# A decoder layer's up projection: products in one line, weights split four ahead, and seven of the 22 output pairs from seven half products in place of eight

## The chip, the cores and the metric

The kernel runs on one core of one Trainium2 chip. The metric is the device time of one execution in microseconds. TensorE (PE) multiplies; PEld is its weight load, which runs beside the multiplies; VectorE (DVE), ScalarE (ACT) and GpSimd (POOL) work on tiles in SBUF, the first two of them also on PSUM; SyncE (SP) issues the DMAs here.

## What is computed

One layer of a hybrid decoder: a mixing sub-layer (three kinds of attention) and a gated MLP with a causal convolution. The change lies in the MLP, in the first of its two matrix products:

```python
h = _rmsnorm(x, norm_ffn[l]) * (1.0 + sc2) + sh2          # (512, 1024)
u = _causal_dwconv(h @ w_up[l], conv_w[l], conv_b[l])     # w_up: 1024 x 5632, conv width 3
u_gate, u_val = jnp.split(u, 2, axis=-1)                  # 2816 columns each
x = x + g2 * ((jax.nn.silu(u_gate) * u_val) @ w_down[l])
```

Everything is float32.

## The kernel before

There are 512 tokens; they are the moving operand of the products, 512 columns at most. The up projection has 44 column blocks of 128; block f of the gate half and block f + 22 of the value half make a pair, and there are 22 pairs (f = 0 to 21).

To keep float32 accuracy each operand is held as a high part in the matmul's own format and a low part, the difference. So each 128x128 weight block costs three matmuls: hi x hi, lo x hi, hi x lo (lines L1290, L1291 and L1293 in `up`). One DMA brings 512 input rows of a block as a tile `w_st` (256 KB); `split_w` makes `w_hi` of it with a cast on ACT (L225) and `w_lo` with a subtraction on POOL (L227), or, where its caller asks for a share, on DVE for every second tile. A pair from f = 2 on has four such tiles and 48 matmuls of 512 columns. The first two pairs (f = 0, 1) work on 256 columns at a time, since the second half of the tokens is not there yet; they are 8 runs of 24 matmuls of 256 columns.

When a block's sum stands in PSUM, `conv` makes the convolution: one ACT operation (L1297) and two on DVE (L1298, L1299), each of which reads PSUM and one SBUF tile. A pair's end is SiLU on ACT (L1325), the product of the two halves on DVE (L1326), a cast `a_hi` on ACT (L1327) and the low part `a_lo` on DVE (L1328). These last two make the moving operand of the down projection. In its f loop the up projection also builds the gate of the residual add (`gate_steps`, L410, 16 operations on DVE in two groups, after f = 4 and f = 8).

The order on each engine is set by a scheduler that plays the program through before it runs; nothing is reordered on the chip between the instructions of DVE, ACT or POOL, so that one that waits holds those behind it. PSUM has 8 banks of 512 columns, handed out in a ring; `w_hi` and `w_lo` have 9 buffers each, `w_st` three, and the working tile `tm` eight.

## Time and profile before

| | us |
|---|---|
| median of 3 runs | 749.01 |
| lowest and highest | 748.26, 753.52 |
| profiled execution, whole | 747.43 |
| its span in the profile | 745.7 |
| busy in the span: PE | 717.4 |
| PEld | 563.3 |
| DVE | 422.4 |
| ACT | 350.5 |
| POOL | 300.1 |

The profiled execution lasted 1.73 us more than its span. Its own time is 1.58 us below the median. The up projection's f loop from pair 2 on starts at 392.51 us of the span; the down projection follows it directly.

### The profile page before, as it was taken

The page shows a single profiled execution, that of the slowest core. Times are in us where ns is not written, and L with a number is a line of the kernel's source. Part 1 is how long each engine was busy: PE and PEld are TensorE (multiplying, and loading weights), DVE is VectorE, ACT ScalarE, POOL GpSimd, SP SyncE. Part 2 cuts the span into 40 slices and gives each one's busy share as a digit, 9 for nine tenths or more (in the row PEclk, how much of TensorE's full clock was granted, in tenths as well). Part 3 has the DMA queues.
Part 4 walks back from the last instruction along what each step waited for, and adds up shares of the span by engine and source line. Part 5 has one row for each costly group of instructions (what it writes and reads, how often), then busy time and mean ns, then how long its engine had stood idle before and what let it go on. Part 6 is the DMA issues. An engine that isn't in the chain of part 4 may idle for free.

```text
span 745.7 us, 11381 instructions
## 1 busy us (share of the span) xinstructions
PE 717.4 (96%) x4224; PEld 563.3 (76%) x4224; DVE 422.4 (57%) x761; ACT 350.5 (47%) x671; POOL 300.1 (40%) x262
## 2 busy tenths in 40 slices
...
GB/s 323 394 165 42 68 19 29 86 100 225 241 193 121 63 123 44 69 46 130 82 100 127 110 178 109 202 102 93 86 102 96 88 107 103 85 99 100 86 13 113
DMA packets 43018, 86.90 MB, mean 117 GB/s; under 512 B 5001, under 2 KB 5203, under 8 KB 42963
## 3 DMA queue, kind: packets, MB, share of 16 engines
...
## 4 chain that ended last, share of the span: by engine, by line
PE 85%; DVE 9%; ACT 2%; issue 1%; DMA 1%; POOL 0%; SPq 0%; DVEq 0%; POOLq 0%; ACTq 0%
PE ch L1290 4%; PE ch L1293 4%; PE ch L1291 4%; PE mm L455 3%; PE at L1290 3%; PE at L1293 3%; PE mm L1290 3%; PE mm L1293 3%; PE at L1291 3%; PE mm L1291 3%; PE mm L456 2%; PE mm L457 2%; PE ch L374 2%; PE ch L1185 2%; PE ch L1184 2%; PE ch L1183 2%
## 5 line engine op out<-in xcount | busy, mean ns | idle before, releaser
L227 POOL TENSOR_TENSOR w_lo<-w_st,w_hi 128x512 fp32r<-128x512 f32 (+1 forms) x164 | 220.1, 1346 | 340.1 <-ACT w_hi L225 318.6
L225 ACT CAST w_hi<-w_st 128x512 fp32r<-128x512 f32 (+1 forms) x184 | 112.9, 617 | 167.9 <-PE at L1185 44.7
L227 DVE TENSOR_TENSOR w_lo<-w_st,w_hi 128x512 fp32r<-128x512 f32 x22 | 16.1, 734 | 83.8 <-ACT w_hi L225 83.8
L1290 PE MATMUL ch<-h_hi,w_hi 128*128 128x512 f32 (+1 forms) x152 | 55.2, 372 | 1.3 <-ACT h_hi L1234 1.3
L1291 PE MATMUL ch<-h_hi,w_lo 128*128 128x512 f32 (+1 forms) x152 | 54.9, 369 | 0.0
L455 PE MATMUL mm<-h_hi,w_hi 128*128 128x512 f32 x104 | 48.8, 469 | 1.8 <-ACT ptr L1017 1.8
L456 PE MATMUL mm<-h_lo,w_hi 128*128 128x512 f32 x104 | 42.2, 406 | 0.0
L457 PE MATMUL mm<-h_hi,w_lo 128*128 128x512 f32 x104 | 42.2, 405 | 0.0
L1290 PE MATMUL at<-h_hi,w_hi 128*128 128x512 f32 (+1 forms) x104 | 36.2, 360 | 0.0
L1291 PE MATMUL at<-h_hi,w_lo 128*128 128x512 f32 (+1 forms) x104 | 36.1, 359 | 0.0
L1293 PE MATMUL ch<-h_lo,w_hi 128*128 128x512 f32 (+1 forms) x152 | 35.0, 371 | 0.0
L1290 PE MATMUL mm<-h_hi,w_hi 128*128 128x512 f32 x88 | 34.7, 394 | 0.0
L1291 PE MATMUL mm<-h_hi,w_lo 128*128 128x512 f32 x88 | 34.6, 393 | 0.0
L1290 PEld LDWEIGHTS ch<-h_hi,w_hi 128*128 128x128 f32 x152 | 28.6, 188 | 7.1 <-ACT h_hi L1234 1.8
L1298 DVE SCALAR_TENSOR_TENSOR tm<-ch,vec,tm 128x511 f32<-128x511 f32 x17 | 12.7, 749 | 36.7 <-ACT tm L1297 36.7
L1291 PEld LDWEIGHTS ch<-h_hi,w_lo 128*128 128x128 f32 x152 | 28.6, 188 | 5.2
L430 DVE SCALAR_TENSOR_TENSOR w_m<-w_m,cB 128x512 f32<-128x512 f32 x32 | 25.8, 831 | 9.7 <-DMA w_m<-in_mod_cols_dram 9.6
L1293 PEld LDWEIGHTS ch<-h_lo,w_hi 128*128 128x128 f32 x152 | 26.7, 188 | 5.5 <-POOL h_lo L1235 0.2
L455 PEld LDWEIGHTS mm<-h_hi,w_hi 128*128 128x128 f32 x104 | 20.3, 195 | 9.0 <-issue 3.1
L1006 ACT ACTIVATE pr<-at,mx 128x128 f32<-128x128 f32 (+3 forms) x32 | 16.9, 527 | 21.6 <-DVE mx L1004 21.1
L1325 ACT ACTIVATE tm<-tm 128x512 f32<-128x512 f32 x22 | 13.9, 633 | 25.6 <-DVE tm L1299 25.6
L1004 DVE TENSOR_REDUCE mx<-at 128x1 f32<-128x128 f32 (+3 forms) x32 | 15.6, 488 | 17.3 <-PE at L1001 17.1
...
## 6 DMA issues: line engine op xcount, KB each, us to landing
w_st<-in_w_up_dram SPq DMA_DIRECT2D x88, 256.0 KB, 2.7
w_st<-in_w_down_dram SPq DMA_DIRECT2D x44, 256.0 KB, 2.6
...
w_m<-in_mod_cols_dram SPq DMA_DIRECT2D x32, 256.0 KB, 3.7
w_st<-in_in_cols_dram SPq DMA_DIRECT2D x30, 256.0 KB, 2.7
w_m<-in_mod_gates_dram SPq DMA_DIRECT2D x16, 256.0 KB, 3.0
w_st<-in_w_out_dram SPq DMA_DIRECT2D x16, 256.0 KB, 2.6
tm<-in_mod_gates_dram SPq DMA_DIRECT2D x16, 256.0 KB, 4.7
```

Source lines behind the costliest of these rows:

```text
L225: (V.tensor_copy if hv[0] else S.copy)(hi[:, :n], st[:, :n])
L227: e.tensor_tensor(lo[:, :n], st[:, :n], f32(hi[:, :n]), op=OP.subtract)
L374: mm(first[j], w[:, P * j:P * j + P], h[:, k, :], start=k == 0 and w is hi and not last, stop=k == NK - 1 and last)
L430: V.scalar_tensor_tensor(wm, wm, 1.0, cB[:, cols], op0=OP.mult, op1=OP.mult, accum_out=acc2[:, z, k, half:half + 1])
L455: mm(out[0], hi[:, z, :], hT_hi[:, k, :], start=k == 0, stop=False)
L456: mm(out[0], hi[:, z, :], hT_lo[:, k, :], start=False, stop=False)
L457: mm(out[0], lo[:, z, :], hT_hi[:, k, :], start=False, stop=k == NK - 1)
L1004: V.reduce_max(mx[:, 0:1], s_ps[:, :n], axis=AX.X, negate=True)
L1006: S.activation(pr[:, :n], s_ps[:, :n], AF.Exp, bias=mx[:, 0:1], accum_out=mx[:, 1:2])
L1290: mm(pu[:, tok], hi[:, k % 4, :], h2_hi[:, k, tok], start=k == 0, stop=False)
L1291: mm(pu[:, tok], lo[:, k % 4, :], h2_hi[:, k, tok], start=False, stop=False)
L1293: mm(pu[:, tok], w[k // 4][0][:, k % 4, :], h2_lo[:, k, tok], start=False, stop=k == NK - 1)
```

## The change

Pairs 0 and 1 stay. From pair 2 on the products become one list of jobs, which PE takes in the order written. A job is 12 matmuls (`product`): one weight tile, split into hi and lo, with four blocks of moving columns. Tiles are fetched seven jobs ahead and split so that, in the program's text, four split tiles are ready ahead of the one in use. The low part is now made on POOL and on DVE in turn (share 2).

Fifteen of the 22 pairs stay as they are in work: pairs 0 and 1, and 13 pairs of four jobs of 512 columns (`jobs_eight`). The other seven (5, 7, 9, 10, 12, 14, 15) are made by `jobs_seven`: the pair is seen as a 2x2 matrix of weight tiles (gate or value block, first or second half of the 1024 inputs) times a 2x2 matrix of token tiles (half of the inputs, half of the tokens), and its four quarter results come from seven products of 256 columns in place of eight. For these, sums and differences are formed:

- of the tokens once, for all seven pairs (`half_sums`): their hi and lo parts lie in four pairs of tiles `s`, `a0`, `a1`, `a2`; its 14 steps stand one behind each of the first 14 jobs;
- of the weights in each pair: four additions of 128x512 on DVE (L1357 of the new kernel), in place in four staging tiles `w_st4`, of which there are four in all; seven tiles are split per pair (one of them twice) where four were;
- of the results in each pair: four copies of 256 columns from PSUM by ACT (L1366, L1378, L1389, L1405), and three additions on DVE of 512, 256 and 256 columns (L1400, L1406, L1407). Products p6, p3 and p7 add onto a PSUM region whose value before must first have been copied out by L1366, L1378 and L1389.

The gate's steps move from behind pairs 4 and 8 to behind pairs 16 and 18.

```diff
+SEVEN = (5, 7, 9, 10, 12, 14, 15)
+NA = 16
+LA = 4
...
+    sums = [[late.tile([P, 4, 256], F32R, name=n + p) for p in ("hi", "lo")] for n in ("s", "a0", "a1", "a2")]
 
     def act_tile(arr, f):
-        return arr[0][:, f, :] if f < NK else arr[1][:, f - NK, :]
+        if f >= NA and len(arr) < 3 + (f - NA) // 2:
+            arr.append(late.tile([P, 2, T], F32R, name=f"a{(f - NA) // 2}" + ("hi" if arr is a_hi else "lo")))
+        return arr[0][:, f, :] if f < NK else arr[1][:, f - NK, :] if f < NA else arr[2 + (f - NA) // 2][:, f % 2, :]
+    def half_sums(c):
+        x = {}
+        def restore(q):
+            for h in range(2):
+                x[q, h] = tm().rearrange("p (k t) -> p k t", k=2)
+                part = (slice(0, P), slice(4 * q + 2 * c, 4 * q + 2 * c + 2), slice(256 * h, 256 * h + 256))
+                V.tensor_tensor(x[q, h], f32(h2_hi[part]), f32(h2_lo[part]), op=OP.add)
+        def combine():
+            V.tensor_tensor(x[0, 0], x[0, 1], x[0, 0], op=OP.subtract)
+            V.tensor_tensor(x[0, 1], x[1, 1], x[0, 1], op=OP.subtract)
+            V.tensor_tensor(x[1, 1], x[1, 1], x[0, 0], op=OP.subtract)
+            V.tensor_tensor(x[1, 0], x[1, 0], x[1, 1], op=OP.subtract)
+        def part(n, t):
+            hi, lo = [z[:, 2 * c:2 * c + 2, :] for z in sums[n]]
+            S.copy(hi, x[t])
+            (G if n % 2 else V).tensor_tensor(lo, x[t], f32(hi), op=OP.subtract)
+        return [lambda: restore(0), lambda: restore(1), combine] + [lambda n=n, t=t: part(n, t) for n, t in
+                                                                   enumerate(((0, 0), (1, 1), (0, 1), (1, 0)))]
+    def product(o, w, x, start):
+        hi, lo = w
+        for k in range(4):
+            mm(o, hi[:, k, :], x[0][k], start=start and k == 0, stop=False, skip_group_check=not start)
+            mm(o, lo[:, k, :], x[0][k], start=False, stop=False, skip_group_check=not start)
+        for k in range(4):
+            mm(o, hi[:, k, :], x[1][k], start=False, stop=k == 3, skip_group_check=not start)
...
+    def jobs_eight(f):
...
+        return [(lambda z=z, q=q: stage(z, q), lambda z=z, q=q: split_w(st.pop((z, q)), 2),
+                 lambda w, z=z, q=q: run(w, z, q)) for z in range(2) for q in range(2)]
+    def jobs_seven(f):
+        st, pu, snap = {}, [], []
+        def stage(z, q):
+            st[z, q] = late.tile([P, T], F32, name="w_st4", bufs=4)
+            dma(st[z, q], w_up[f + NF * z, q])
+        def parts(z, q):
+            return split_w((st[z, q], 4, T), 2)
+        def add(o, a, b, op=OP.subtract):
+            V.tensor_tensor(st[o], st[a], st[b], op=op)
+        h0, h1 = slice(0, 256), slice(256, 512)
+        a11, a12, a21, a22 = (0, 0), (0, 1), (1, 0), (1, 1)
+        def p1(w):
+            pu.extend(bank(next(ring)) for z in range(3))
+            snap.extend(tm() for z in range(2))
+            product(pu[1][:, h1], w, tokens(0, 0), True)
+            S.copy(snap[0][:, h0], pu[1][:, h1])
+        def p2(w):
+            product(pu[0][:, h0], w, tokens(1, 0), True)
+        def s5():
+            add(a11, a11, a21)
+            add(a21, a21, a22, OP.add)
+            return parts(*a21)
+        def p5(w):
+            product(pu[0][:, h1], w, combined(0), True)
+            S.copy(snap[1][:, h1], pu[0][:, h1])
+        kept22 = []
+        def s6():
+            kept22.append(parts(*a22))
+            add(a22, a22, a11)
+            return parts(*a22)
+        def p6(w):
+            product(pu[1][:, h1], w, combined(1), False)
+            S.copy(snap[0][:, h1], pu[1][:, h1])
+        def p4(w):
+            product(pu[2][:, h0], kept22[0], combined(3), True)
+        def s3():
+            add(a12, a12, a22)
+            return parts(*a12)
+        def p3(w):
+            product(pu[0][:, h1], w, tokens(1, 1), False)
+            V.tensor_tensor(pu[0], pu[0], snap[0], op=OP.add)
+            us[f].append(conv(pu[0], f))
+        def p7(w):
+            product(pu[1][:, h1], w, combined(2), False)
+            S.copy(snap[1][:, h0], pu[1][:, h1])
+            V.tensor_tensor(pu[1][:, h1], pu[1][:, h1], snap[1][:, h1], op=OP.add)
+            V.tensor_tensor(pu[1][:, h0], pu[2][:, h0], snap[1][:, h0], op=OP.add)
+            us[f].append(conv(pu[1], f + NF))
+        us[f] = []
+        none = lambda: None
+        return [(lambda: (stage(*a11), stage(*a12)), lambda: parts(*a11), p1), (lambda: stage(*a21), lambda: parts(*a12), p2),
+                (lambda: stage(*a22), s5, p5), (none, s6, p6), (none, none, p4), (none, s3, p3),
+                (none, lambda: parts(*a11), p7)]
...
-    for f in range(NF):
-        if f == 0:
...
-        else:
-            us = []
-            for z in (f, f + NF):
-                pu = bank(next(ring))
-                up(pu, up_weights(z), slice(0, T))
-                us.append(conv(pu, z))
...
-        if f in (4, 8):
-            for g in gate_steps(1, f // 8, tm, tm):
-                g()
...
+    jobs, side = [], []
+    for f in range(FG, NF):
+        mine = (jobs_seven if f in SEVEN else jobs_eight)(f)
+        jobs += [(*j, f if n == len(mine) - 1 else None) for n, j in enumerate(mine)]
+    for c in range(2):
+        side += half_sums(c)
+    staged, ready = 0, {}
+    with tc.manual_schedule(engines=MENG):
+        for n, (_, _, run, f) in enumerate(jobs):
+            while staged < min(len(jobs), n + LA + 3):
+                jobs[staged][0]()
+                staged += 1
+            while len(ready) < min(len(jobs), n + LA + 1):
+                ready[len(ready)] = jobs[len(ready)][1]()
+            run(ready[n])
+            ready[n] = None
+            if side:
+                side.pop(0)()
+            if f is None:
+                continue
+            gated(f)
...
+            if f in (16, 18):
+                for g in gate_steps(1, f // 18, tm, tm):
+                    g()
+            if f in (17, 19):
+                gate_parts(1, f // 19, tm)
+            if f in (18, 20):
+                gate_end(1, f // 20, bank(next(ring)), g2b)
```

In the new kernel the lines of `split_w` are L229 (cast, ACT) and L231 (low part), those of `conv` L1437 to L1439, and those of a pair's end L1444 to L1447; the matmuls are L1315, L1316 and L1318.

How the order moves, at two places. The first is ACT around the end of a pair: before, from the convolution of pair 8's value block on.

```order
L1297 ACTIVATE tm_4856<-pv_4819,vec2_108 128x512
L225 CAST w_hi_5068<-w_st_5066 128x512
L1327 CAST a_hi_3953<-tm_4856 128x512
L225 CAST w_hi_5074<-w_st_5072 128x512
L225 CAST w_hi_5109<-w_st_5107 128x512
L1297 ACTIVATE tm_4926<-ch_4889,vec2_108 128x512
```

In the new kernel, from the convolution of pair 8's value block (`tm_5028`) on; pair 9 is the first of two neighbours made from seven products, `mm_5036` and `ch_5037` are its PSUM banks, and the `w_st4` tiles 5054 to 5094 are the weights of pair 10.

```order
L1437 ACTIVATE tm_5028<-ch_4994,vec2_108 128x512
L229 CAST w_hi_5113<-w_st4_5056 128x512
L1366 COPY tm_5039<-ch_5037 128x256
L229 CAST w_hi_5131<-w_st4_5075 128x512
L229 CAST w_hi_5152<-w_st4_5094 128x512
L1446 CAST a_hi_3953<-tm_5028 128x512
L1378 COPY tm_5040<-mm_5036 128x256
L229 CAST w_hi_5157<-w_st4_5094 128x512
L1389 COPY tm_5039<-ch_5037 128x256
L229 CAST w_hi_5205<-w_st4_5056 128x512
```

The cast `a_hi` of pair 8 waits for DVE's L1445, and now stands ahead of the copies out of PSUM (L1378, L1389) for which PE's later products of pair 9 wait.

The second place is DVE ahead of pair 5, the first with seven products. Before, on pair 3:

```order
L1298 SCALAR_TENSOR_TENSOR tm<-at,vec_108,tm 128x511
L1299 SCALAR_TENSOR_TENSOR tm<-at,vec_108,tm 128x510
L1298 SCALAR_TENSOR_TENSOR tm<-mm,vec_108,tm 128x511
L1299 SCALAR_TENSOR_TENSOR tm<-mm,vec_108,tm 128x510
L1326 TENSOR_TENSOR tm<-tm 128x512
L1328 TENSOR_TENSOR h_lo<-tm,h_hi 128x512
```

In the new kernel, on pair 4, up to the low parts of the second half of the token sums (`slo`, `a1lo`; 47 rows, one of them of two operations, lead from the first L1295 to the last `slo`):

```order
L1439 SCALAR_TENSOR_TENSOR tm<-mm,vec_108,tm 128x510
L1295 TENSOR_TENSOR tm<-h_hi,h_lo 128x512
L1445 TENSOR_TENSOR tm<-tm 128x512
L1299 TENSOR_TENSOR tm<-tm 128x512
L231 TENSOR_TENSOR w_lo<-w_st_4414,w_hi 128x512
L1447 TENSOR_TENSOR h_lo<-tm,h_hi 128x512
L1300 TENSOR_TENSOR tm<-tm 128x512
L1438 SCALAR_TENSOR_TENSOR tm<-ch,vec_108,tm 128x511
L1301 TENSOR_TENSOR tm<-tm 128x512
L1439 SCALAR_TENSOR_TENSOR tm<-ch,vec_108,tm 128x510
L1302 TENSOR_TENSOR tm<-tm 128x512
L1307 TENSOR_TENSOR slo<-tm,shi 128x512
```

Between the operations on PSUM stand now the sums (L1295 to L1302), the low parts of weights (L231) and of token sums (L1307), all of which read two tiles in SBUF; the product p5 of pair 5 reads `slo`.

## Rows read from the trace of the kernel before

**Rows 1.** The page: busy time, share of the span and instructions of each engine.

```profile
PE 717.4 (96%) x4224; PEld 563.3 (76%) x4224; DVE 422.4 (57%) x761; ACT 350.5 (47%) x671; POOL 300.1 (40%) x262
```

**Rows 2.** Busy time of each engine in 20 us of the up projection.

```profile
core 0: us, PE busy (x) PEld busy (x) DVE busy (x) ACT busy (x) POOL busy (x), PEclk, DMA share, GB/s
...
520.00:540.00 20.00, 20.00 (x88) 16.21 (x87) 7.47 (x10) 9.53 (x16) 9.35 (x8) 1.00 0.29 90
```

**Rows 3.** Waits of PE from 360 us to the end: total us, times, longest us.

```profile
PE mm L1222 <- ACT tm L1230: 1.6, 1, 1.6
PE ch L1290 <- ACT h_hi L1234: 1.3, 1, 1.3
```

**Rows 4.** Timeline of PE: first 512-column matmuls of two outputs with one between (start, us).

```profile
442.63 0.40 PE L1290 MATMUL ch<-h_hi,w_hi 128*128 128x512 f32 x1
...
453.75 0.40 PE L1290 MATMUL mm<-h_hi,w_hi 128*128 128x512 f32 x1
```

**Rows 5.** Timeline of PE: first matmuls of three 256-column runs, and of pair 2.

```profile
384.03 0.28 PE L1290 MATMUL ch<-h_hi,w_hi 128*128 128x256 f32 x1
...
386.83 0.28 PE L1290 MATMUL at<-h_hi,w_hi 128*128 128x256 f32 x1
...
389.67 0.28 PE L1290 MATMUL at<-h_hi,w_hi 128*128 128x256 f32 x1
...
392.51 0.39 PE L1290 MATMUL mm<-h_hi,w_hi 128*128 128x512 f32 x1
```

**Rows 6.** DVE's groups, 395 to 597 us: count | busy us, mean ns | idle before.

```profile
L1326 DVE TENSOR_TENSOR tm<-tm 128x512 f32<-128x512 f32 x19 | 15.3, 803 | 0.7
L410 DVE SCALAR_TENSOR_TENSOR tm<-tm,cact 128x512 f32<-128x512 f32 x14 | 14.0, 1003 | 4.3 <-DMA tm<-in_mod_gates_dram 4.0
L1298 DVE SCALAR_TENSOR_TENSOR tm<-ch,vec,tm 128x511 f32<-128x511 f32 x13 | 9.7, 749 | 26.9 <-ACT tm L1297 26.9
...
L1328 DVE TENSOR_TENSOR a_lo<-tm,a_hi 128x512 fp32r<-128x512 f32 x11 | 7.6, 692 | 7.2 <-ACT a_hi L1327 7.2
...
L1328 DVE TENSOR_TENSOR h_lo<-tm,h_hi 128x512 fp32r<-128x512 f32 x7 | 5.5, 788 | 5.7 <-ACT h_hi L1327 5.7
...
L417 DVE TENSOR_TENSOR tm<-tm 128x512 fp32r<-128x512 f32 x2 | 1.4, 693 | 0.1
```

**Rows 7.** POOL's only group in the same stretch.

```profile
L227 POOL TENSOR_TENSOR w_lo<-w_st,w_hi 128x512 fp32r<-128x512 f32 x74 | 97.8, 1324 | 104.2 <-ACT w_hi L225 103.8 <-PE mm L1293 0.4
```

**Rows 8.** ACT's groups in the same stretch.

```profile
L225 ACT CAST w_hi<-w_st 128x512 fp32r<-128x512 f32 x74 | 45.5, 615 | 42.9 <-PE ch L1293 15.2 <-PE mm L1293 11.0 <-PE at L1293 9.3
...
L1297 ACT ACTIVATE tm<-mm,vec 128x512 f32<-128x512 f32 x10 | 7.8, 776 | 1.9 <-PE mm L1293 1.9
...
L1327 ACT CAST a_hi<-tm 128x512 fp32r<-128x512 f32 x11 | 6.8, 621 | 21.7 <-DVE tm L1326 21.7
```

**Rows 9.** Timeline of POOL, 476 to 483 us.

```profile
476.54 3.00 POOL L227 TENSOR_TENSOR w_lo<-w_st,w_hi 128x512 fp32r<-128x512 f32 x2 [2.74 <-ACT w_hi L225]
482.10 1.30 POOL L227 TENSOR_TENSOR w_lo<-w_st,w_hi 128x512 fp32r<-128x512 f32 x1 [2.56 <-ACT w_hi L225]
```

**Rows 10.** Timeline of DVE in the same stretch.

```profile
478.63 3.03 DVE L410 SCALAR_TENSOR_TENSOR tm<-tm,cact 128x512 f32<-128x512 f32 x3 [0.25 <-DMA tm<-in_mod_gates_dram]
481.58 0.74 DVE L1298 SCALAR_TENSOR_TENSOR tm<-ch,vec,tm 128x511 f32<-128x511 f32 x1
482.24 1.71 DVE L410 SCALAR_TENSOR_TENSOR tm<-tm,cact 128x512 f32<-128x512 f32 x1
```

**Rows 11.** ACT's 256-column copy out of PSUM, whole span.

```profile
L1122 ACT COPY KR<-ch 128x256 f32<-128x256 f32 x8 | 3.0, 370 | 3.5 <-PE ch L1120 3.3
```

**Rows 12.** DVE's 256-column operation on PSUM and SBUF, whole span.

```profile
L918 DVE TENSOR_TENSOR KR<-KR,ch 128x256 f32<-128x256 f32 x8 | 3.3, 418 | 1.3 <-PE ch L917 1.2
```

**Rows 13.** DMA issues of the page: KB each, median us to landing.

```profile
w_st<-in_w_up_dram SPq DMA_DIRECT2D x88, 256.0 KB, 2.7
```

**Rows 14.** Waits, 395 to 620 us: total us, times, longest us.

```profile
ACT a_hi L1327 <- DVE tm L1326: 25.6, 13, 2.1
```

More of the change, by code (lines that the diff above doesn't have):

```diff
@@ new lines, in product, with tokens @@
+    def product(o, w, x, start):
[5 more added lines that the diff above has]
+            mm(o, hi[:, k, :], x[1][k], start=False, stop=k == 3, skip_group_check=not start)
+    def tokens(q, h):
+        sl = slice(256 * h, 256 * h + 256) if h < 2 else slice(0, T)
+        return [[z[:, 4 * q + k, sl] for k in range(4)] for z in (h2_hi, h2_lo)]
@@ new lines, in combined, with run @@
+    def combined(n):
+        return [[z[:, k, :] for k in range(4)] for z in sums[n]]
+    def jobs_eight(f):
+        pu, st = [], {}
+        def stage(z, q):
+            st[z, q] = stage_w(w_up[f + NF * z, q], 4)
+        def run(w, z, q):
+            if q == 0:
+                pu.append(bank(next(ring)))
+            product(pu[z], w, tokens(q, 2), q == 0)
+            if q == 1:
+                us[f].append(conv(pu[z], f + NF * z))
+        us[f] = []
+        return [(lambda z=z, q=q: stage(z, q), lambda z=z, q=q: split_w(st.pop((z, q)), 2),
+                 lambda w, z=z, q=q: run(w, z, q)) for z in range(2) for q in range(2)]
@@ L1278, in cvec @@
+    us = {}
     def cvec(w, f):
```

46 lines of the change are left out of this document (22 added, 24 removed).

## Prediction

> **What bounds the kernel now.** I read the page first, then the stages. PE is busy 717.4 of the span [rows 1], and the 20 us windows of the up projection say more: in the one shown PE is busy 20.00 of 20.00 us at a granted clock of 1.00, its upper level, DVE 7.47, ACT 9.53, POOL 9.35 [rows 2]; the ten other windows between 400 and 620 us read the same for PE. The list of waits has for PE, from 360 us to the end, two entries of 1.6 and 1.3 us, both in the normalization ahead of pair 0 [rows 3]. So from pair 2 to the end of the up projection PE waits for nothing. A better order or an earlier split can win nothing there; only fewer PE columns can, and any new wait of PE is a loss in full.
>
> **What PE saves.** Durations of single matmuls overlap, so I take start to start. In the 512-column form one pair, two outputs and 48 matmuls, takes 453.75 - 442.63 = 11.12 us [rows 4]. Three 256-column runs follow each other at 2.80, 2.84 and 2.84 us for 24 matmuls each [rows 5], so 12 take 1.41 us; the weight load for each matmul is in that. Seven products are 84 such matmuls, 7 x 1.41 = 9.87 us, in place of 11.12: 1.25 us per pair, 8.75 us for seven. The other 13 pairs keep their 48 matmuls. Nothing else on PE changes but the place of the gate's four matmuls.
>
> **What the other engines get.** Prices are from [rows 6]: an operation with a PSUM input as L1298 0.75 us; one with two SBUF tiles 0.69 (the 692 of L1328, the 693 of L417), which I take for the additions L1357, L1295 to L1302 and the low parts too. The 512-column addition onto PSUM I also take at 0.69, the 256-column ones at 0.42 [rows 12]. A pair of seven products then asks of DVE: four additions and on average 3.5 low parts (5.2), four convolution operations (3.0), L1445 and L1447 (1.4), and L1400, L1406, L1407 (1.5): 11.1 us against 9.87 of PE. A pair of eight asks 2 x 0.69 + 3.0 + 1.4 = 5.8 against 11.12. ACT: seven casts of 0.62, four copies of 0.37 [rows 11], two convolutions of 0.78, SiLU and `a_hi` of 0.62 each [rows 8]: 8.6 us. POOL: 3.5 x 1.32 = 4.6 us [rows 7]. Over pairs 5 to 15 all engines fit below PE (DVE 7 x 11.1 + 4 x 5.8 = 101 against 7 x 9.87 + 4 x 11.12 = 114), so the gain isn't lost on average. It can be lost locally, at two kinds of place.
>
> **The head: token sums ahead of pair 5.** Product p5 of pair 5 starts 3 x 11.12 + 2 x 1.41 = 36.2 us after pair 2 does, and reads `slo`, whose second half is the last of the 47 rows in front of it on DVE. They are 48 operations: 12 on PSUM (9.0 us) and 36 with two SBUF tiles (24.8), 33.8 together. By the order ahead of them DVE comes to the first about 0.5 us after pair 2 starts, so it would be done at 34.3, in time by 1.9 us, if it never waited. ACT and POOL have less to do in this stretch.
>
> **The neighbours 9 and 10, 14 and 15.** Both pairs use the same four `w_st4` tiles. The first weight of pair 10 can be fetched only when the last split of pair 9 has read its tile, some 3 us before pair 9's first product (call that time 0), and lands 2.7 us later [rows 13]; DVE's row for it starts at about 0.9. From there I follow DVE's 17 rows up to pair 9's L1407: ten with two SBUF tiles (6.9), four of the convolution (3.0), L1400, L1406 and L1407 (1.5), 11.4 us of work, and 2.4 us in which it waits for the later landings, for casts and for PE. On the way L1445 of pair 8 ends at 6.65; ACT's cast `a_hi`, which waits for DVE already today (25.6 us in all, up to 2.1 [rows 14]), ends at 7.3 and the copy L1378 behind it at 7.7, where PE wants to start p3 at 7.05: PE loses 0.7. L1407 ends at 14.7; ACT's convolution and the copy L1366 behind it end at 16.1, where p6 of pair 10 would start at 14.8: 1.3 more. A neighbour costs 2.0 us in this way, and pairs 5, 7 and 12, which have a pair of eight behind them, none: there DVE has fallen behind by 1.2 us and gains 5.3 in the next pair.
>
> **The shared price, DVE beside POOL.** The timelines show one effect that this sum lacks. POOL is busy from 476.54 to 479.54; of three L410 from 478.63 on, 0.75 us each in the undisturbed case, all three take 3.03. The L410 at 482.24 takes 1.71, with a POOL operation from 482.10 to 483.40; L1298 at 481.58, beside none, takes 0.74 [rows 9, 10], and L1298's mean of 749 shows that operations with a PSUM input hardly ever lose time though POOL is busy half of the window [rows 6, 7]. So a DVE operation with two SBUF tiles waits for the POOL operation in flight. How much is that per operation? L1326, L1328 and L417, all tensor_tensor, lose 19 x 0.11 + 7 x 0.10 over 39 operations, 0.07 each; L410, which stands in rows of its own kind, loses 0.25 (1003 against some 750) [rows 6]. These are my bounds, with zero below. I take 0.07, since the added operations are tensor_tensor too. The head then ends at 34.3 + 36 x 0.07 = 36.9, 0.7 late; of the ten rows in a neighbour six lie ahead of the first late copy, 0.4 us, so 2.4 or 2.5 each.
>
> The Trainium skill ("SBUF — State Buffer", Who interferes with whom) says that a VectorE instruction with two SBUF inputs contends with a GpSimd instruction that reads SBUF, and that the later one blocks for the whole of the other. The 1.71 us of L410 agree. By that rule at its hardest, with operations that arrive without regard to each other, the price per operation would be nearer to the upper bound than to 0.07: the second rival below.
>
> **The sum.** 8.75 of gain, less 0.7 at the head and 2 x 2.5 at the neighbours: 3.0 us. From the profiled execution, 747.4 - 3.0 = 744.4; the median stands 1.6 above that execution, so 746.0. I predict 746.
>
> **Smaller parts at nothing.** The gate's steps behind pairs 16 and 18: 16 operations there raise DVE to 11.5 + 16 x 0.75 to 1.0 = 23.5 to 27.5 us over two pairs of 22.2, but the splits are 11 us ahead and pairs 20 and 21 give the rest back; uncovered it would cost up to 5. Loads on SP: 88 as before, of the same size. A PSUM bank is taken again two to three pairs later, far behind the convolution that frees it. The splits on POOL fall from four to two or 3.5 per pair, and no wait of PE for POOL is there to be removed.
>
> **Rivals.** *The gain arrives whole.* DVE's order has enough slack at the head, and the late copies are not late, because landings come earlier or DVE is less behind than I count. For it: the slack of 1.9 us at the head, and averages that fit. Against it: pairs of seven at 11.1 us of DVE, twice in a row. Time: 749.0 - 8.75 = 740.3.
>
> *DVE and POOL block each other, and the change costs time.* At 0.25 per operation the head ends at 34.3 + 9.0 = 43.3, 7.1 late; a neighbour has 19 operations with two SBUF tiles, 4.8 us more, 6.8 in all, since DVE is the last one in the chain throughout. Sum 7.1 + 13.6 = 20.7, less 8.75: 12 us slower, 761. In general the loss is 74e + 2.1 for a price e; it eats the gain at e = 0.09 and makes the kernel slower by 1% at 0.19. For it: L410's 0.25 is from the only stretch in which DVE runs such operations back to back. Against it: the mean of 0.07 in the same window, and a PE that waits lets DVE catch up.
>
> *The change doesn't do what it says.* The seven products could need more PE time than counted if 256-column matmuls ran slower off the first pairs; [rows 5] speak against that, and I give it nothing.
>
> **Chances.** 1% is 7.5 us, about what a measurement here can tell from no change. Forecast and its neighbourhood, losses of 1.3 to 16 us: 0.60. The gain nearly whole, below 741.5: 0.27. Slower by over 1%, above 756.5: 0.13. The range reaches from the whole gain with the spread of the runs (749.0 against 748.3) below it, 739.5, up to 757, where the second rival begins to decide; some 0.12 is left out above and a little below.
>
> **What the profile will show.** PE's windows between pair 5 and 15 fall below 20.00 by 4 to 8 us in all. PE waits for ACT copies (L1378, L1366) in pairs 9, 10, 14 and 15, and for `slo` or its neighbours at pair 5. Seven-product pairs without a wait take 9.9 us. DVE is busy over 90% there, and its operations with two SBUF tiles stand above 0.69 in the mean, by 0.07 if I am right, by 0.2 or more if the rival is. Wrong would be a PE that waits for weights (`w_hi`, `w_lo`) through many pairs, or for a bank of PSUM.

## The result, and the profile after

The changed kernel takes 755.73 us (median of 10 runs, 752.91 to 760.27), the kernel before 749.30 in runs beside it: a ratio of 1.0087, 95% interval 1.0065 to 1.0108. I had forecast 746.0, a small gain; it is a loss of 6.4 us, inside the range and on the other side of zero.

The page of the changed kernel, its span and its busy times, answers to [rows 1]:

```profile
span 755.2 us, 12022 instructions
PE 718.0 (95%) x4476; PEld 577.6 (76%) x4476; DVE 510.2 (68%) x880; ACT 371.6 (49%) x728; POOL 271.1 (36%) x237
```

PE is as busy as before, although it has 8.75 us less to multiply (3.9 us of this busy time lie ahead of pair 2: 375.3 there after, 371.4 before). The place is found by the stretch from pair 2's first matmul to the down projection's first. Its window before the change, with busy times (and counts) of PE, PEld, DVE, ACT and POOL, then PE's granted clock:

```profile
392.50:616.10 223.60, 223.60 (x966) 181.19 (x965) 111.25 (x147) 102.07 (x163) 103.92 (x79) 1.00 0.40 117
```

and after, where windows inside the stretch answer to [rows 2]:

```profile
396.00:625.40 229.40, 220.16 (x1219) 191.69 (x1218) 196.19 (x264) 123.11 (x219) 78.93 (x56) 0.98 0.36 110
430.00:440.00 10.00, 7.00 (x56) 6.45 (x54) 9.96 (x11) 5.19 (x10) 6.38 (x4) 1.00 0.22 60
440.00:450.00 10.00, 7.19 (x32) 6.85 (x33) 7.37 (x10) 4.77 (x10) 4.08 (x3) 0.66 0.36 107
540.00:550.00 10.00, 7.49 (x50) 7.29 (x49) 9.14 (x15) 6.24 (x13) 5.86 (x4) 0.83 0.04 14
```

The stretch should have come down to 223.6 - 8.75 = 214.9; it is 229.4. The down projection behind it takes 129.6 and 129.8 us. (The two spans differ by 9.5, not 5.8: 3.5 us arise ahead of pair 2, where the code is the same. Over the profiled executions of this document pair 2 starts anywhere from 391.5 to 399.0 us, so stretches are compared and not spans. The difference of the medians, 6.4, goes with the stretch.) The missing 14.5 us are of two kinds. First, PE stands still for 229.4 - 220.2 = 9.2 us, where before it never did. The list of its waits in the stretch answers to [rows 3] (total, times, longest):

```profile
PE pv L1315 <- ACT tm L1378: 4.0, 1, 4.0
PE at L1315 <- ACT tm L1378: 2.5, 1, 2.5
PE pv L1318 <- DVE slo L1307: 1.8, 1, 1.8
PE ch L1315 <- ACT tm L1366: 0.9, 1, 0.9
```

They are in pairs 5, 14, 5 and 10. Second, behind the waits of 4.0 and 2.5 us the granted clock falls, and the two 10 us windows above read 0.66 and 0.83. PE's timeline answers to [rows 5]: 443.41 and 443.84 are two matmuls apart in pair 5, 0.215 us for each, 547.88 and 557.81 are the starts of pair 15 and of pair 16.

```profile
443.41 0.41 PE L1315 MATMUL pv<-h_hi,w_hi 128*128 128x256 f32 x1
443.84 0.41 PE L1315 MATMUL pv<-h_hi,w_hi 128*128 128x256 f32 x1
...
547.88 0.28 PE L1315 MATMUL ch<-h_hi,w_hi 128*128 128x256 f32 x1
...
557.81 0.39 PE L1315 MATMUL mm<-h_hi,w_hi 128*128 128x512 f32 x1
```

So an undisturbed pair of seven takes 9.93 us, as priced (9.87), and a matmul behind the wait of 4.0 us takes 0.215 in place of 0.118: the lower of the two levels, 1.2 in place of 2.4 GHz. Worked out from windows of 1 us, the granted clock is 0.50 from 441.7 to 448.5 and from 544.1 to 547.5; PE is back at work from 442.81 on in pair 5 and throughout in pair 14.

An experiment below (e14_hold) runs the same matmuls with no wait in 215.0 us; here PE is busy 220.2, and 215.0 + 9.2 + 5.2 = 229.4. Of the 5.2 about 4.5 are the clock's, half of the 9.1 us that PE worked at 0.50. The other 0.7 fits what a wait costs beyond its listed length, some 0.25 us each time while PE's run of matmuls ends and starts again; rows of e11_sums_dve below show it at a clock of 1.00.

**What makes DVE late.** DVE's groups in the stretch answer to [rows 6] (busy us, mean ns):

```profile
L231 DVE TENSOR_TENSOR w_lo<-w_st,w_hi 128x512 fp32r<-128x512 f32 x52 | 42.9, 826 | 6.4 <-ACT w_hi L229 6.3
L1357 DVE TENSOR_TENSOR w_st<-w_st,w_st 128x512 f32<-128x512 f32 x28 | 22.3, 795 | 5.8 <-POOL w_lo L231 3.2 <-DMA w_st<-in_w_up_dram 2.1
L1445 DVE TENSOR_TENSOR tm<-tm 128x512 f32<-128x512 f32 x20 | 20.9, 1047 | 0.3
L1438 DVE SCALAR_TENSOR_TENSOR tm<-ch,vec,tm 128x511 f32<-128x511 f32 x16 | 11.9, 744 | 4.3 <-ACT tm L1437 4.3
```

Operations with two SBUF tiles, priced at 0.69 + 0.07, take 0.80 to 1.05; L1438, which reads PSUM, its usual 0.74. In pair 5 one sees why. DVE's timeline (start, duration), then POOL's, as in [rows 9, 10]:

```profile
433.47 1.76 DVE L1307 TENSOR_TENSOR slo<-tm,shi 128x512 fp32r<-128x512 f32 x1
435.15 1.77 DVE L1307 TENSOR_TENSOR a1lo<-tm,a1hi 128x512 fp32r<-128x512 f32 x1
436.84 1.80 DVE L231 TENSOR_TENSOR w_lo<-w_st,w_hi 128x512 fp32r<-128x512 f32 x1
```

```profile
433.02 1.65 POOL L1307 TENSOR_TENSOR a0lo<-tm,a0hi 128x512 fp32r<-128x512 f32 x1 [1.28 <-ACT a0hi L1306]
434.64 1.73 POOL L1307 TENSOR_TENSOR a2lo<-tm,a2hi 128x512 fp32r<-128x512 f32 x1
436.33 1.76 POOL L231 TENSOR_TENSOR w_lo<-w_st,w_hi 128x512 fp32r<-128x512 f32 x1
```

Each of the three ends about 0.5 us behind the POOL operation that was running when it began, and the POOL operations, 1.32 before [rows 7], are longer too: the two engines go in lockstep, at 1.7 us a piece. The Trainium skill ("SBUF — State Buffer", Who interferes with whom) says that a VectorE instruction with two SBUF inputs contends with a GpSimd instruction that reads SBUF, over a pair of ports that is an exclusive lock; these rows agree.

**How it reaches PE.** SP's loads in pair 5 and its longest wait there (430 to 440 us), then ACT's casts and copies:

```profile
438.66 5.06 SPq L220 DMA_DIRECT2D w_st<-in_w_up_dram  x4
```

```profile
SPq L220 <- DVE w_lo L231: 6.5, 1, 6.5
```

```profile
441.35 0.62 ACT L229 CAST w_hi<-w_st 128x512 fp32r<-128x512 f32 x1 [5.18 <-DMA w_st<-in_w_up_dram]
441.88 0.61 ACT L1446 CAST h_hi<-tm 128x512 fp32r<-128x512 f32 x1
442.40 0.36 ACT L1378 COPY tm<-pv 128x256 f32<-128x256 f32 x1
```

DVE's L231, the last of its three rows above, stands behind the two slow sums and holds a staged weight until it ends at 438.64; the load that waits 6.5 us for this goes out on SP at 438.66 (POOL's L231, done at 438.09, isn't what it waits for). ACT's cast waits 5.2 us for that load, and the copy for which PE waits 4.0 us stands behind the cast. In pair 14 it goes as the prediction had it: the neighbour's weight comes 2.1 us late for DVE (first row), L1445 ends at 542.44, and in ACT's rows the cast `a_hi` and the copy L1378 stand behind it:

```profile
538.81 0.69 DVE L1357 TENSOR_TENSOR w_st<-w_st,w_st 128x512 f32<-128x512 f32 x1 [2.12 <-DMA w_st<-in_w_up_dram]
...
541.46 0.98 DVE L1445 TENSOR_TENSOR tm<-tm 128x512 f32<-128x512 f32 x1
```

```profile
542.47 0.62 ACT L1446 CAST a_hi<-tm 128x512 fp32r<-128x512 f32 x1 [1.79 <-DVE tm L1445]
543.00 0.37 ACT L1378 COPY tm<-at 128x256 f32<-128x256 f32 x1
```

### The profile page after: what moved, and what is told of

Same layout as the page of the kernel before. It is cut to its first block, busy times and chain, and to the rows that moved or that the text cites. A ratio compares the mean times of both kernels' runs of the same rounds, so it can differ in the third digit from the quotient of the medians.

```text
span 755.2 us, 12022 instructions
## 1 busy us (share of the span) xinstructions
PE 718.0 (95%) x4476; PEld 577.6 (76%) x4476; DVE 510.2 (68%) x880; ACT 371.6 (49%) x728; POOL 271.1 (36%) x237
## 4 chain that ended last, share of the span: by engine, by line
PE 70%; DVE 17%; ACT 5%; issue 3%; DMA 2%; POOL 1%; SPq 0%; DVEq 0%; ACTq 0%; POOLq 0%
PE mm L459 3%; PE mm L460 2%; PE mm L461 2%; PE ch L378 2%; PE ch L1315 2%; PE ch L1316 2%; PE ch L1188 2%; PE ch L1318 2%; PE ch L1187 2%; PE ch L1189 2%; DVE w_m L434 2%; DMA w_st<-in_w_up_dram 2%; PE mm L378 2%; PE mm L1318 1%; PE mm L1315 1%
## 5 line engine op out<-in xcount | busy, mean ns | idle before, releaser
L231 POOL TENSOR_TENSOR w_lo<-w_st,w_hi 128x512 fp32r<-128x512 f32 (+1 forms) x135 | 184.9, 1375 | 371.3 <-ACT w_hi L229 347.0
L229 ACT CAST w_hi<-w_st 128x512 fp32r<-128x512 f32 (+1 forms) x205 | 124.9, 618 | 159.6 <-PE ch L1189 46.0
L231 DVE TENSOR_TENSOR w_lo<-w_st,w_hi 128x512 fp32r<-128x512 f32 x72 | 57.8, 803 | 84.2 <-ACT w_hi L229 84.2
L459 PE MATMUL mm<-h_hi,w_hi 128*128 128x512 f32 x104 | 49.1, 472 | 1.8 <-ACT ptr L1021 1.8
L461 PE MATMUL mm<-h_hi,w_lo 128*128 128x512 f32 x104 | 42.5, 408 | 0.0
L1315 PE MATMUL ch<-h_hi,w_hi 128*128 128x512 f32 (+1 forms) x104 | 37.6, 369 | 0.0
L1316 PE MATMUL ch<-h_hi,w_lo 128*128 128x512 f32 (+1 forms) x104 | 37.3, 366 | 0.0
L1315 PE MATMUL mm<-h_hi,w_hi 128*128 128x512 f32 (+1 forms) x96 | 31.9, 347 | 0.0
L1316 PE MATMUL mm<-h_hi,w_lo 128*128 128x512 f32 (+1 forms) x96 | 31.9, 346 | 0.0
L1357 DVE TENSOR_TENSOR w_st<-w_st,w_st 128x512 f32<-128x512 f32 x28 | 22.3, 795 | 5.8 <-POOL w_lo L231 3.2
L1318 PE MATMUL ch<-h_lo,w_hi 128*128 128x512 f32 (+1 forms) x104 | 25.6, 368 | 0.0
L461 PEld LDWEIGHTS mm<-h_hi,w_lo 128*128 128x128 f32 x104 | 20.5, 197 | 5.0
L1315 PE MATMUL at<-h_hi,w_hi 128*128 128x512 f32 (+1 forms) x56 | 21.2, 383 | 2.5 <-ACT tm L1378 2.5
L1445 DVE TENSOR_TENSOR tm<-tm 128x512 f32<-128x512 f32 x22 | 22.3, 1015 | 0.8 <-ACT tm L1444 0.4
L1315 PEld LDWEIGHTS ch<-h_hi,w_hi 128*128 128x128 f32 x104 | 19.7, 189 | 3.7
L460 PEld LDWEIGHTS mm<-h_lo,w_hi 128*128 128x128 f32 x104 | 20.7, 199 | 2.4
L1316 PEld LDWEIGHTS ch<-h_hi,w_lo 128*128 128x128 f32 x104 | 19.7, 189 | 3.6
```

The lines of the kernel that those rows point to most:

```text
L229: (V.tensor_copy if hv[0] else S.copy)(hi[:, :n], st[:, :n])
L231: e.tensor_tensor(lo[:, :n], st[:, :n], f32(hi[:, :n]), op=OP.subtract)
L459: mm(out[0], hi[:, z, :], hT_hi[:, k, :], start=k == 0, stop=False)
L460: mm(out[0], hi[:, z, :], hT_lo[:, k, :], start=False, stop=False)
L461: mm(out[0], lo[:, z, :], hT_hi[:, k, :], start=False, stop=k == NK - 1)
L1315: mm(o, hi[:, k, :], x[0][k], start=start and k == 0, stop=False, skip_group_check=not start)
```

## The experiments

The theory: DVE's operations with two SBUF tiles and POOL's low parts block each other, DVE falls behind, and the lateness reaches PE through the queues of SP and ACT. The rivals: the line and the splits themselves, the order of the loads, copies into the same PSUM halves, and POOL's hold on the staged weights without any blocking. All of them in one table; us is the median; each ratio is to runs of the kernel before made beside that run, whose medians are 748.3 to 749.8; stretch, waits and DVE are of one profiled execution each. "before" is the profiled run on record, "stretch" is from pair 2's first matmul to the down projection's, "waits" the part of it in which PE stood still, DVE its busy time in it.

| run | us | ratio to before, 95% | stretch | waits | DVE |
|---|---|---|---|---|---|
| before | 749.30 | | 223.6 | 0 | 111.3 |
| after | 755.73 | 1.0087 [1.0065, 1.0108] | 229.4 | 9.2 | 196.2 |
| e1_all_eight | 749.90 | 1.0002 [0.9978, 1.0026] | 223.4 | 0 | 133.3 |
| e2_sp_order | 752.89 | 1.0031 [1.0006, 1.0057] | 226.5 | 8.1 | 191.8 |
| e3_fresh | 753.44 | 1.0044 [1.0017, 1.0070] | 227.4 | 8.9 | 190.0 |
| e4_pool_zero | 739.45 | 0.9854 [0.9818, 0.9891] | 214.9 | 0 | 170.6 |
| e5_pool_busy | 739.42 | 0.9881 [0.9848, 0.9915] | 214.9 | 0 | 171.0 |
| e13_read_other | 748.10 | 0.9982 [0.9948, 1.0015] | 221.4 | 4.1 | 186.7 |
| e14_hold | 740.60 | 0.9898 [0.9861, 0.9936] | 215.0 | 0 | 171.1 |
| e6_apart | 742.68 | 0.9937 [0.9914, 0.9960] | 217.4 | 0 | 182.3 |
| e7_apart_dve | 742.77 | 0.9930 [0.9895, 0.9964] | 217.3 | 0 | 184.1 |
| e8_seven_dve | 745.47 | 0.9950 [0.9923, 0.9978] | 220.9 | 3.9 | 192.7 |
| e9_dve_sp | 746.66 | 0.9992 [0.9965, 1.0018] | 220.9 | 4.1 | 193.3 |
| e10_moved | 748.54 | 0.9994 [0.9970, 1.0017] | 222.9 | 5.8 | 194.9 |
| e11_sums_dve | 744.72 | 0.9949 [0.9921, 0.9977] | 219.2 | 2.9 | 193.7 |
| e12_eight | 743.85 | 0.9934 [0.9906, 0.9963] | 218.0 | 2.9 | 195.0 |

### Parts of the change

**e1_all_eight**: the new line, no pair of seven, no token sums.

```diff
-SEVEN = (5, 7, 9, 10, 12, 14, 15)
+SEVEN = ()
...
-        side += half_sums(c)
+        side += []
```

> All 20 pairs from pair 2 on from four products of 512 columns, no token sums; the one line of jobs, the split four ahead and the low parts in turn on POOL and DVE stay. The stretch from pair 2's first matmul to the down projection's first took 223.6 us before and 229.4 after the change. Theory A (PE loses by waiting for copies and sums that stand in queues, and by the granted clock after such waits): PE waits for nothing, stretch 223.6 within 0.5, time within 0.3% of before. Rival C (the line or the shared low parts cost by themselves): stretch over 225.

The time of before, and no wait of PE: the line, the splits four ahead and the low parts shared by DVE and POOL cost nothing. All of the loss belongs to the seven products and the sums made for them.

**e2_sp_order**: SP's loads in the order of the code.

```diff
-    with tc.manual_schedule(engines=MENG):
+    with tc.manual_schedule(engines=MENG | {mybir.EngineType.SP}):
```

> The DMA queue too takes the loads in the order written, so that pair 6's last weight no longer stands behind pair 7's four staging tiles. Theory A: ACT's 5.2 us wait for that load goes, with it the 4.0 us of PE in pair 5 and the half clock behind them (2.8 us); the 1.8 us for slo and the 2.5 us of pair 14 stay: stretch 222 to 224. Rival B (DVE, held by POOL, is simply too late; what ACT waits for is no matter): the wait moves to another row, stretch over 227.

The wait of 4.0 us is gone, but others take its place (L1378 2.9, 1.2 and 1.0, L1366 2.1, `a2lo` 0.9; sum 8.1). It recovers 2.9 of the 14.5 us: the order of loads decides where the lateness surfaces, and it isn't its source.

**e3_fresh**: p3 and p6 are moved to other halves of PSUM banks, so that p3, p6 and p7 should need no copy first.

```diff
-            product(pu[0][:, h1], w, tokens(1, 1), False)
+            product(pu[2][:, h1], w, tokens(1, 1), True)
...
-            product(pu[1][:, h1], w, combined(1), False)
-            S.copy(snap[0][:, h1], pu[1][:, h1])
+            product(pu[1][:, h0], w, combined(1), True)
+            S.copy(snap[0][:, h1], pu[1][:, h0])
```

> Products p3, p6 and p7 write to halves of PSUM banks that are free, in place of adding onto earlier values, so PE need not wait for the copies; the sums of the products are left incomplete. Everything else runs, the copies too. Theory A: PE's waits of 4.0, 2.5 and 0.9 us go and both falls of the clock, the 1.8 us for slo stays: stretch 217 to 219, the kernel about 1.5% below the changed one. Rival B: PE then waits for weights that DVE and POOL have not split, stretch over 222.

A miss, and the edit does less than it says. Only p3 is freed. PE now waits for L1389 three times, 5.6 us in all, at p7, and 1.4 us for L1366 at p6, although these copies read the other half of the bank that p7 and p6 write; the rows show that the order is kept for the whole bank. The longest:

```profile
441.65 0.38 PE L1315 MATMUL ch<-a1hi,w_hi 128*128 128x256 f32 x1 [3.38 <-ACT tm L1389]
```

The wait for `slo` stays at 1.8. Whatever stands on ACT behind a late cast is late; to remove one such copy moves the wait to the next. The run doesn't say what the kernel would take if PE waited for no copy.

### POOL's reads

**e4_pool_zero**

```diff
-        e.tensor_tensor(lo[:, :n], st[:, :n], f32(hi[:, :n]), op=OP.subtract)
+        if e is G and len(wpools) > 1 and share == 2 and nkt == 4:
+            G.memset(f32(lo[:, :n]), 0.0)
+        else:
+            e.tensor_tensor(lo[:, :n], st[:, :n], f32(hi[:, :n]), op=OP.subtract)
```

> POOL's low parts of weights (every second tile of the up projection) are set to zero in place of subtracted, so POOL reads no SBUF there; the low part of these tiles is left out. Rival B (DVE is late because POOL's reads hold it): DVE's operations with two SBUF tiles fall from 0.80 to 1.05 us to 0.70, the wait for slo goes, and the waits for copies shrink below 2 us together: stretch 217 to 221. Theory A without B (queue order alone): the 4.0 us of pair 5 shrink by less than half, stretch over 224.

**e5_pool_busy**: the same with

```diff
-            G.memset(f32(lo[:, :n]), 0.0)
+            for _ in range(3):
+                G.memset(f32(lo[:, :n]), 0.0)
```

> In place of each of POOL's subtractions in the pairs of seven, and in the pairs of eight between them, POOL sets the same low part to zero three times: it reads no SBUF tile, but is busy for about 3 x 0.53 = 1.58 us, longer than the subtraction (1.39 in the changed kernel). Left out: the low part of every second tile of the up projection. Theory A (DVE's operations with two SBUF tiles are held up by POOL's reading operation): as in the run with one zeroing, pair 2 to the down projection near 215 us, DVE's low parts near 0.71, PE hardly waits, 739 to 741 us. Theory B (POOL's own time in the chain from weight to product, and the order in the queues, is what was missing): as the changed kernel or worse, 227 to 230 us for the stretch, waits for ACT's copies as before, 752 to 757 us.

Both stretches are 214.9, the whole of the 8.75 us, and PE waits for nothing. POOL is busy 39.8 us in the one and 89.4 in the other, more than in the changed kernel (78.9): its busy time doesn't matter. But both take two things away at once, the reads beside DVE and POOL's hold on the staged weight: a zeroing waits for no cast, and SP may load the tile again at once. Two more runs separate these.

**e13_read_other**: the reads without the hold. POOL subtracts a resident tile from itself.

```diff
-            G.memset(f32(lo[:, :n]), 0.0)
+            other = f32(h2_hi[:, 0, :])
+            e.tensor_tensor(lo[:, :n], other, other, op=OP.subtract)
```

> In place of the low part of every second tile of the up projection (left out, as in the two runs that zeroed it) POOL subtracts one resident tile of tokens from itself: an operation of the same form and length, 1.32 to 1.4 us, that reads SBUF beside DVE but holds no staged weight and waits for no cast. Theory A (the blocking itself makes DVE late): DVE's low parts back at 0.80 to 0.85, additions at 0.78 to 0.85, L1445 at 0.9 to 1.05, PE waits of 5 to 10 us for copies and sums, stretch 225 to 230, 751 to 757. Theory D (what the zeroing took away was the hold: POOL's operation no longer waits for the cast, and frees the staged tile at once, so SP loads early): stretch 214.5 to 217, 739 to 742, whatever DVE's durations are. Between 218 and 224 both have a part.

**e14_hold**: the hold without the reads.

```diff
-            G.memset(f32(lo[:, :n]), 0.0)
+            e.tensor_tensor(lo[:, :16], st[:, :16], f32(hi[:, :16]), op=OP.subtract)
+            for _ in range(2):
+                e.memset(f32(lo[:, 16:n]), 0.0)
+            e.tensor_tensor(lo[:, :16], st[:, :16], f32(hi[:, :16]), op=OP.subtract)
```

> The opposite: POOL waits for the cast, subtracts the first 16 columns, sets the rest to zero twice (about 1.06 us without a read of SBUF), and subtracts 16 columns again, so that the staged tile is held about as long as by the whole subtraction. Left out: the rest of the low part of every second tile of the up projection. Theory A: DVE's operations at 0.69 to 0.75, stretch 214.5 to 217.5, 739 to 742. Theory D: the waits for copies in pairs 5 and 14 as in the changed kernel, stretch 225 to 230, 751 to 757, with DVE's operations short all the same.

DVE's groups in the stretch of e13_read_other (lines stand 4 further on: L235 is L231, L1361 is L1357, L1449 is L1445, L1382 is L1378), then its POOL group and its PE waits:

```profile
L235 DVE TENSOR_TENSOR w_lo<-w_st,w_hi 128x512 fp32r<-128x512 f32 x52 | 41.2, 793 | 5.0 <-ACT w_hi L229 4.5 <-issue 0.2
L1361 DVE TENSOR_TENSOR w_st<-w_st,w_st 128x512 f32<-128x512 f32 x28 | 25.1, 897 | 3.3 <-DMA w_st<-in_w_up_dram 2.7
L1449 DVE TENSOR_TENSOR tm<-tm 128x512 f32<-128x512 f32 x20 | 16.9, 847 | 0.3
```

```profile
L233 POOL TENSOR_TENSOR w_lo<-h_hi 128x512 fp32r<-128x512 f32 x47 | 59.5, 1270 | 120.6 <-PE ch L1320 39.8 <-PE mm L1320 35.1 <-PE pv L1320 23.3
```

```profile
PE at L1319 <- ACT tm L1382: 2.2, 1, 2.2
PE pv L1319 <- ACT tm L1382: 1.9, 1, 1.9
```

and of e14_hold (6 lines further on), DVE's groups and the POOL groups:

```profile
L237 DVE TENSOR_TENSOR w_lo<-w_st,w_hi 128x512 fp32r<-128x512 f32 x52 | 36.6, 704 | 7.3 <-ACT w_hi L229 6.9 <-PE ch L1322 0.2
L1363 DVE TENSOR_TENSOR w_st<-w_st,w_st 128x512 f32<-128x512 f32 x28 | 19.3, 690 | 5.9 <-POOL w_lo L235 4.0 <-DMA w_st<-in_w_up_dram 1.4
L1451 DVE TENSOR_TENSOR tm<-tm 128x512 f32<-128x512 f32 x20 | 13.7, 686 | 0.3
```

```profile
L234 POOL MEMSET w_lo<- 128x496 f32 x96 | 48.9, 513 | 65.6 <-PE ch L1322 22.0 <-PE mm L1322 17.7 <-PE pv L1322 13.4
L232 POOL TENSOR_TENSOR w_lo<-w_st,w_hi 128x16 fp32r<-128x16 f32 x48 | 14.3, 297 | 37.0 <-ACT w_hi L229 36.7
```

With the hold alone the stretch is 215.0: POOL waits for casts as before, additions wait for it 4.0 us, and nothing of that reaches PE. With the reads alone DVE is slow again (0.79 to 0.90), and the stretch is 221.4, between the bounds that I had set: 4.1 us of waits and 2.3 of slower work of PE behind them. With both it is 229.4. So the blocking is needed for any loss, and reads that hold nothing are enough for 6.4 us.

The 8.0 us between this run and the changed kernel are not taken apart, and aren't simply POOL's hold. POOL's operations also fall at other times here: they wait for PE to be done with `w_lo`, and no longer for the cast. And DVE's sums of pair 5, in lockstep with POOL in the changed kernel (`slo` 1.76), run undisturbed here, and the wait for `slo` is gone:

```profile
427.90 0.68 DVE L1311 TENSOR_TENSOR slo<-tm,shi 128x512 fp32r<-128x512 f32 x1
```

### The place of the pairs and of the low parts

**e6_apart** and **e7_apart_dve**

```diff
-SEVEN = (5, 7, 9, 10, 12, 14, 15)
+SEVEN = (7, 9, 11, 13, 15)
```

> Five pairs of seven products, 7, 9, 11, 13 and 15, with a pair of eight between any two and two more pairs ahead of the first, so that no pair of seven's weights wait for the tiles of the pair just ahead, and the token sums have 22 us more. Theory A (blocking makes DVE late, and the lateness reaches PE only where a second pair of seven or the sums stand close behind): 5 x 1.25 = 6.25 us less PE time and few waits, stretch 217.5 us, 743 to 745. Theory C (one pair of seven alone makes DVE late enough): waits for L1378 or L1366 of 0.5 to 2 us in most of the five pairs and a lower clock behind them, 748 to 752.

and for the second, all low parts of pairs of seven on DVE:

```diff
-            return split_w((st[z, q], 4, T), 2)
+            return split_w((st[z, q], 4, T), 1)
```

> The same five pairs, and in them every low part on DVE, POOL only in the pairs of eight. DVE gets 3.5 operations more per pair of seven, 11.1 + 2.4 = 13.5 us against 9.87 of PE, and the pair of eight behind gives back 5.3. Theory A: DVE's operations in pairs of seven fall to 0.69 to 0.72, DVE is late by 3.6 us at the end of a pair and level again after the next, no long PE wait, 743 to 745. Theory C: DVE is late by more than the casts and copies have slack, waits for L1378 of 1 us or more in each of the five, 749 to 754.

217.4 and 217.3: the full 6.25 us, no wait. In e6_apart DVE's low parts take 0.81 and L1445 0.88, so the blocking is nearly as dear as in the changed kernel, and yet PE never waits. That fits theory A, by which DVE recovers in the pair of eight behind; but the first pair of seven also stands two pairs later, further from the sums, and the run doesn't tell these two apart. Whether the low parts are on POOL or DVE makes no difference then.

**e8_seven_dve**: the second edit alone, at the seven pairs of the change.

> The changed kernel with every low part of the seven pairs of seven on DVE; POOL works only in the pairs of eight and for two of the token sums. Over pairs 5 to 15 DVE has 7 x 13.5 + 4 x 5.8 = 117.7 us against 113.6 of PE. Theory A (blocking): operations of 0.69 to 0.72 in place of 0.80 to 1.05, which about pays for the 24.5 operations more; DVE is late by some 4 us over the eleven pairs and most at 9/10 and 14/15: 746 to 753, not slower than the changed kernel. Theory B (no blocking, DVE's operations are long for a reason of their own): 24.5 operations more at 0.83 on the engine that is late, 20 us more of DVE, most of it on PE's path: 765 to 775.

The stretch is 220.9 although DVE has 25 low parts more, and DVE is busy less (192.7 against 196.2); L231 takes 0.73. No wait at 9/10 nor at 14/15. One is left, 3.9 us for L1389 in pair 5. POOL's timeline there:

```profile
427.50 4.09 POOL L1307 TENSOR_TENSOR a0lo<-tm,a0hi 128x512 fp32r<-128x512 f32 x1 [17.63 <-ACT a0hi L1306]
431.56 1.74 POOL L1307 TENSOR_TENSOR a2lo<-tm,a2hi 128x512 fp32r<-128x512 f32 x1
433.26 1.75 POOL L231 TENSOR_TENSOR w_lo<-w_st,w_hi 128x512 fp32r<-128x512 f32 x1
```

**e9_dve_sp** (e8 with e2's edit) and **e10_moved** (e8 with SEVEN = (7, 9, 10, 12, 14, 15, 17)).

> The pairs of the changed kernel, every low part of a pair of seven on DVE, and SP's loads in the order in which the code names them. With all low parts on DVE one PE wait was left, 3.9 us in pair 5, where ACT's copy L1389 stands behind casts whose weights' loads stand on SP behind a load that waits for its tile. If SP's order is the cause of that one, it goes: stretch 215 to 217 us, no wait above 1 us, 740 to 742.5 us. If DVE's lateness at pair 5 is the cause, the wait stays at 3 to 4 us whatever SP does: stretch 220 to 222, 745 to 747.

> Seven pairs of seven again, with every low part of theirs on DVE and SP's order left to the scheduler, but from pair 7 on: 7, 9, 10, 12, 14, 15 and 17 in place of 5, 7, 9, 10, 12, 14 and 15. The token sums and the loads for the first of them have 20 us more. If the wait of 3.9 us belongs to pair 5 (the sums, casts and loads that meet there): stretch 215 to 217, 740 to 742.5 us. If it belongs to the first pair of seven wherever it stands (its loads and the next pair's meet on SP in the same way): again one wait of 3 to 4 us, now in pair 7, and 745 to 747; a wait in pair 17 by the gate's steps would give the same time, with another place.

The order on SP changes nothing: the wait is 4.1 us, and my first reading of e8's pair 5, an order on SP, falls. Moved, the first pair of seven has no wait, so it belongs to pair 5, where the sums are made. The new wait is in pair 17, by the gate's steps: ACT's copy needs a `tm` tile that L414 still reads; this and the clock behind it (0.68 from 560 to 570 us) make 748.5, somewhat above what I had written for it.

```profile
561.86 0.37 ACT L1366 COPY tm<-at 128x256 f32<-128x256 f32 x1 [3.45 <-DVE tm L414]
```

**e11_sums_dve** (e8, and the sums' low parts on DVE) and **e12_eight** (the same with pair 21 as an eighth).

```diff
-            (G if n % 2 else V).tensor_tensor(lo, x[t], f32(hi), op=OP.subtract)
+            V.tensor_tensor(lo, x[t], f32(hi), op=OP.subtract)
```

> As the run with all low parts of the pairs of seven on DVE, at the same pairs, and the low parts of the token sums on DVE too, so that POOL has only low parts of pairs of eight. Theory: in pair 5 a low part of a pair of eight stood on POOL behind two sums that wait for ACT (until 427 us in the last runs), its tile came free late (434.5), SP and with it ACT's cast and copy waited for that. Then the wait of 3.9 us goes: stretch 215 to 217.5 us, no PE wait above 1 us, 740 to 743 us. Rival (DVE itself is late at pair 5, as the prediction had it): two more operations per step on DVE make it later, the wait stays or becomes one for a sum, 3 to 6 us: stretch 220 to 223, 745 to 748.

> The same with pair 21, the last one, as an eighth pair of seven; the gate's steps are over by then. If the stretch is bound by PE: 1.25 us less than the run beside it, stretch 213.5 to 216.5, 739 to 742. If the longer end of a pair of seven (a copy and two additions ahead of the convolution) holds up the down projection, the two are equal or this one is up to 3 us slower.

The wait of 3.9 is gone. PE's waits in e11_sums_dve, and its timeline around one of them, with the starts of two products of pair 10 and of the next:

```profile
PE ch L1315 <- ACT tm L1366: 2.0, 2, 1.2
PE ch L1315 <- ACT tm L1389: 0.5, 1, 0.5
PE mm L1315 <- ACT tm L1378: 0.4, 1, 0.4
```

```profile
480.80 0.28 PE L1315 MATMUL mm<-shi,w_hi 128*128 128x256 f32 x1
...
483.56 0.39 PE L1315 MATMUL ch<-a0hi,w_hi 128*128 128x256 f32 x1 [1.19 <-ACT tm L1366]
...
485.09 0.28 PE L1315 MATMUL at<-a2hi,w_hi 128*128 128x256 f32 x1
```

So in pair 5 of e8 a pair of eight's low part on POOL had stood behind two sums, slow by blocking, and held its tile; SP's longest wait there, 4.1 us, is for it. In the changed kernel the low part behind two sums was DVE's; the path is the same.

The stretch, 219.2, is 1.7 above what I expected: the four waits of 2.9 us, in pairs 7, 10, 12 and 15, and 1.4 of PE's busy time, though the granted clock reads 1.00 from end to end. The two products above take 4.29 us in place of 2 x 1.42 = 2.84, 1.45 more around a listed wait of 1.19: each wait costs some 0.25 beyond its length. The eighth pair brings 1.2 us more in the stretch. e6_apart, e7_apart_dve and e12_eight, at 0.993 to 0.994 of before, beat both kernels and can't be told apart; e8 and e11, at 0.995, lie within their intervals.

## Why the prediction was wrong

Term by term: the head was put at 0.7 us and measured 1.8; the two neighbours at 5.0 and measured 3.4; all else at nothing, and measured 4.0 (a second wait in pair 5) and 5.2 (PE slower behind its waits). That is 14.5 of losses, with rounding, against 5.7. The steps that failed are the last two; below them lies the price of a blocked operation, without which nothing is lost.

**PE saves 1.25 us per pair of seven: right.** The stretch without waits is 214.9 or 215.0 against 223.6 - 8.75 = 214.9; five pairs give 6.2.

**The shared price, 0.07 us per operation: mis-sized, 0.16 measured.** In the stretch DVE is busy 196.2 us, and 171.1 in e14_hold, which runs as many operations without POOL's long reads. There are 156 with two SBUF tiles: 52 L231, 28 L1357, 20 L1445, 20 L1447, 14 L414, 4 L1307, 2 L421 and 16 of L1295 to L1302. That is 25.1 / 156 = 0.16 us each, between my bounds of 0 and 0.25. In my own sum it gives 3.9 at the head and 3.0 at each neighbour, 9.8 in all, enough to turn the gain into a loss of 1.0. I took 0.07 from operations that before stand alone, with idle time around them [rows 6]; the ones added stand in a row, where each meets POOL's next operation. The row that was like them was L410's 0.25 [rows 6, 10], and I gave its rival 0.13. Some of the error went the other way: three DVE operations in a row, as at 543.07, 543.68 and 544.28, start 0.60 apart, and I counted 0.69.

**The head, 0.7 us by `slo`: the right place, 1.8 in size.** 1.1 of it is the single operation at 433.47 that took 1.76.

**The neighbours, 2.5 us each: the mechanism right in 14/15, the sizes not.** 14/15 lost 2.5 by L1378 and nothing by L1366; 9/10 lost 0.9 by L1366 and nothing by L1378.

**"Pairs 5, 7 and 12 none", and the loads "at nothing": wrong for pair 5.** Its 4.0 us are the largest wait. I had followed DVE's rows only up to `slo`. Two rows on, DVE's low part L231 was late too, and through the tile that it held the lateness went to SP's load, to ACT's cast and to the copy L1378. In the kernel with the low parts on DVE, e10_moved and e11_sums_dve show that the wait in pair 5 is tied to the sums; for the changed kernel the rows of pair 5 say so, and no run tests it alone.

**The clock: not foreseen, 4.5 us, and 0.7 at the ends of the waits.** I counted a wait of PE at its length. Behind the waits of 4.0 and 2.5 us PE worked at the lower clock, which gave away two thirds as much again.

**The second rival** had the cause, blocking, at a price below its 0.25 and with a path and a clock that it didn't name. Its formula (loss 74e + 2.1) gives 13.9 at 0.16, near the 14.5 measured, but by luck: it puts 10.1 at the neighbours, where 3.4 was lost, and has no clock. For e13_read_other, where the same division gives (186.7 - 171.1) / 156 = 0.10, it gives 9.5, and 6.5 was lost. That DVE would be over 90% busy was right around pair 5 only (9.96 of 10 us); over the whole stretch it is 86% (196.2 of 229.4).

What stays open: what makes up the 8.0 us between e13_read_other and the changed kernel, and why e11_sums_dve still waits 2.9 us, in four products; no run takes these apart.
